# Every fourth piece of weights gets its low part from an accumulating DMA in a float32 encoder layer

## The chip, the cores and the metric

The kernel runs on one core of one Trainium2 chip. The metric is the device time of one execution in microseconds (us). The kernel before was timed twice: 2108.68 and 2109.56 us, median 2109.12 us.

## The reference

One encoder layer over 256 tokens of width 2048, all in float32:

```python
h = x + 0.5 * rms_norm(swiglu(rms_norm(x)))          # w_gate, w_up: 2048 x 5632, w_down: 5632 x 2048
u = rms_norm(h); q, k, v, f, g = split(u @ w_in)     # w_in: 2048 x 8192
y_attn = attention(q, k, v) @ w_attn_o               # 16 query heads, 4 key heads, rotary, head norms
y_four = real(fft2(f)) @ w_fourier                   # 8 groups of 128 channels
h = h + rms_norm((sigmoid(g_A) * y_attn + sigmoid(g_B) * y_four) @ w_out)
y = h + 0.5 * rms_norm(swiglu(rms_norm(h)))          # a second feed-forward half-step
```

Nearly all the work is in the matrix products with the weights: about 386 MB of float32 weights are read once, and each is used for 256 tokens.

## The kernel before, in words

**Precision.** TensorE multiplies in a format (fp32r) that keeps fewer bits than float32. So every operand is split in two: `hi` is the value rounded to fp32r, `lo` is what the rounding left. A product is three matmuls into one PSUM bank, hi by hi, hi by lo, lo by hi (`mm3`, lines 97 to 100; the weights' `lo` is the operand of line 99).

**Pieces of weights.** Weights are cut into chunks of 4 k-tiles by 512 columns, and a chunk into two pieces of 2 k-tiles: 128 partitions by 1024 float32 values, 512 KB. `piece` (line 104) loads a piece into a tile `raw` by a DMA of SyncE (SP), takes a `hi` and a `lo` tile, and calls `split` (line 92): ScalarE (ACT) copies `raw` to `hi` with rounding (line 93), then VectorE (DVE) writes `raw - hi` to `lo` (line 94). So `hi` and `lo` are ready one after the other, and `raw` is free when VectorE is done.

**Room.** There are 5 buffers for `raw` (`RAW_BUFS`) and 6 each for `hi` and `lo` (`RING`), used in turn. ScalarE can split a piece only when its load has landed and TensorE is done with the piece six places earlier. SP issues its DMAs in one queue, in order; the load of a piece waits until the `raw` buffer of the piece five places earlier is free, and the loads behind it in the queue wait with it.

**Stages.** `col_block` (line 179) computes 512 columns of u @ w for both tiles of 128 tokens: each piece serves 2 k-tiles by 2 token tiles by 3 matmuls, 12 matmuls in a row. `row_block` (line 209) adds ch @ w for one chunk, token tile 0 first and then token tile 1, so that the two pieces of a chunk are both used twice, 24 matmuls for the two. `ffn` (line 395) alternates two column blocks (gate, up) and a row block (down), 11 times. The mixers between the two half-steps use the same blocks.

**The two transitions.** At the end of the first half-step and of the mixers, `last_rows` (line 219) computes the last row block for token tile 0, then for token tile 1 while the norms of tile 0 run, then the first column block of what follows: token tile 0 while the norms of token tile 1 run, then token tile 1. The order on VectorE is written out by hand there. Part of the weights goes to spare room instead of the ring (`SPARE`, `SPARE_NEXT`); of the next column block's four chunks the first goes to a large buffer (tile names `wh`, `wl`), and the chunks 1 to 3 to the ring. Two pieces of these matter below: the first piece of chunk 1, and the first piece of chunk 3. Names there: `junk` are ScalarE's squares for the norms (line 336), `ca` to `cr` VectorE's steps of an inverse root (lines 148 to 159), `uh`, `ul` the split of the transposed next input, `pt` the PSUM tile of a transpose, `pc` and `pr` the PSUM tiles of a column and a row block. GpSimd (POOL) does only the products of the norms with their gains (line 337).

The order of instructions on each engine is set when the kernel is built: by the order of the code, by priorities of a scheduler for ScalarE, SP and TensorE, and by hand for VectorE in `last_rows`.

Of the kernel before, what the change touches and what calls it, by code (L numbers as in the profile page):

```python
# [10 lines left out]
F32 = mybir.dt.float32  # L11
# [3 lines left out]
AF = mybir.ActivationFunctionType  # L15
# [16 lines left out]
EPS = 1e-6  # L32
# [7 lines left out]
B8 = 8  # L40
CH = 3
WARM = 8
BY_POOL = ()


@with_exitstack
def encoder_layer(
# [41 lines left out]

    latest = {}  # L90

    def split(hi, lo, src):
        a = A.activation(hi, src, AF.Copy)  # L93
        v = V.tensor_tensor(out=lo, in0=src, in1=hi.bitcast(F32), op=ALU.subtract)  # L94
        latest["A"], latest["V"] = a.ins, v.ins
# [6 lines left out]
    ident = const.tile([P, P], F32, name="ident")  # L102

    def piece(src, k0, n, pools=None):
        """k-tiles k0 .. k0 + n of a chunk of weights: raw, hi, lo."""
        shape, part = [P, WP, NB], slice(0, n)
        raw = wraw.tile(shape, F32, tag="raw", name="raw")[:, part, :]
        load(raw, src.rearrange("p (k c) -> p k c", k=CK)[:, k0:k0 + n, :])
        pl, th, tl = pools or (wring, "hi", "lo")
        hi = pl.tile(shape, F32R, tag=th, name="whi")[:, part, :]  # L110
        lo = pl.tile(shape, F32R, tag=tl, name="wlo")[:, part, :]
        split(hi, lo, raw)
        return [(hi[:, k, :], lo[:, k, :]) for k in range(n)]

    def pieces(src, spare=None):
        """A chunk of weights, piece by piece: functions that load one and give (hi, lo) of its k-tiles.
        spare: the pool to take room from instead of the ring."""
        whole = {}

        def part(k0):  # L120
            if spare in (None, "chunk"):
                return piece(src, k0, WP, (chunk, "ch_hi", "ch_lo") if spare else None)
            if not whole:
                for c in ("h", "l"):
                    shape = [P, CK, NB]
                    whole[c] = big("w" + c, F32R, shape) if spare == "b8" else \
                        upool.tile(shape, F32R, tag=f"u{c}1", name=f"w{c}u")
            raw = wraw.tile([P, WP, NB], F32, tag="raw", name="raw")
            load(raw[:], src.rearrange("p (k c) -> p k c", k=CK)[:, k0:k0 + WP, :])
            hi, lo = (whole[c][:, k0:k0 + WP, :] for c in "hl")  # L130
            split(hi, lo, raw[:])
            return [(hi[:, j, :], lo[:, j, :]) for j in range(WP)]

        return [lambda k0=k0: part(k0) for k0 in range(0, CK, WP)]

    def weights(src, spare=None):
        """A chunk of weights as (hi, lo) of its k-tiles."""
        return [t for load_part in pieces(src, spare) for t in load_part()]

    def rsqrt_steps(ssq, n, inv, name, mult=1.0, pre=None):  # L140
        """mult / sqrt(ssq * inv + EPS), or of ssq * inv + pre: a step of third order and one of second."""
        up = (8.0 / 3.0 / mult) ** 2
        a, y, t, w, q, z, t2, w2, r = (small(name + c, n) for c in "aytwqzuvr")
        i = sm.tile([P, n], I32, tag="smi" + str(n), name=name + "i")
        if pre is None:
            yield r, V.tensor_scalar(out=a[:], in0=ssq, scalar1=inv * up, scalar2=EPS * up, op0=ALU.mult, op1=ALU.add)
        else:
            yield r, V.scalar_tensor_tensor(out=a[:], in0=ssq, scalar=inv * up, in1=pre, op0=ALU.mult, op1=ALU.add)
        yield r, V.tensor_scalar(out=i[:], in0=a[:].bitcast(I32), scalar1=1, scalar2=None, op0=ALU.logical_shift_right)
        yield r, V.tensor_scalar(out=y[:].bitcast(I32), in0=i[:], scalar1=-1.0, scalar2=float(0x5F3759DF),  # L150
                                 op0=ALU.mult, op1=ALU.add)
        yield r, V.tensor_tensor(out=t[:], in0=y[:], in1=y[:], op=ALU.mult)
        yield r, V.tensor_tensor(out=w[:], in0=t[:], in1=a[:], op=ALU.mult)
        yield r, V.scalar_tensor_tensor(out=q[:], in0=w[:], scalar=-10.0 / 3.0, in1=w[:], op0=ALU.add, op1=ALU.mult)
        yield r, V.scalar_tensor_tensor(out=z[:], in0=q[:], scalar=5.0, in1=y[:], op0=ALU.add, op1=ALU.mult)
        yield r, V.tensor_tensor(out=t2[:], in0=z[:], in1=z[:], op=ALU.mult)
        yield r, V.scalar_tensor_tensor(out=w2[:], in0=t2[:], scalar=-0.5 * 9.0 / 64.0, in1=a[:],
                                        op0=ALU.mult, op1=ALU.mult)
        yield r, V.scalar_tensor_tensor(out=r[:], in0=w2[:], scalar=1.5, in1=z[:], op0=ALU.add, op1=ALU.mult)

    def rsqrt(*args, **kw):
        for r, _ in rsqrt_steps(*args, **kw):
            pass
        return r
# [12 lines left out]
        return tuple(upool.tile([P, KD, P], F32R, tag=f"u{c}{t}", name=f"u{c}{t}") for c in "hl")  # L177

    def col_block(u, w, nb, between=()):
        """u @ w[nb] for both token tiles: PSUM tiles. between: pieces of other work, spread over the block."""  # L180
        ps = [pmm.tile([P, NB], F32, tag="mm", name="pc") for _ in range(NT)]
        step = KD / (len(between) + 1)
        done = 0
        for kg in range(KD // CK):
            wt = weights(w[nb, kg])
            for k in range(CK):
                kk = kg * CK + k
                if done < len(between) and kk >= (done + 1) * step:
                    if between[done]:
                        with tc.issue_after(mm.ins):  # L190
                            between[done]()
                    done += 1
                for t in range(NT):
                    mm = mm3(ps[t][:], u[t][0][:, kk, :], u[t][1][:, kk, :], *wt[k], kk == 0, kk == KD - 1)
        return ps
# [11 lines left out]
        return mm  # L207

    def row_block(ch, w, rb, y, first, between=()):
        """y += ch @ w[rb]; between[cb] comes ahead of column block cb."""  # L210
        for cb in range(D // NB):
            wt = weights(w[rb, cb])
            if cb < len(between) and between[cb]:
                with tc.issue_after(mm.ins):
                    between[cb]()
            for t in range(NT):
                mm = row_part(ch, wt, t, cb, y, first)

    def last_rows(ch, w, rb, y, norm, nxt=None, w_next=None):
        """The last row block, token tile 0 first, and the norms behind it; then the first column block of what  # L220
        follows, its token tile 0 while token tile 1 gets ready. VectorE's order is given: it has the most to do here."""
        ws = [weights(w[rb, cb], spare=SPARE[cb]) for cb in range(D // NB)]

        def row(t, cb):
# [92 lines left out]
        return a[:, cb * NB:(cb + 1) * NB]  # L317

    class PostNorm:
        """h += half * rms_norm(y) * g_post per token tile."""  # L320

        def __init__(self, y, h, g_post, half, store=None):
            self.y, self.h, self.g, self.half, self.store = y, h, g_post, half, store
# [35 lines left out]
                self.store(t, *self.parts[i])  # L359

    class NextInput:
        """u = transpose(h * g_pre), rs[t] = rsqrt(mean(h^2)); y is room."""

        def __init__(self, y, h, g_pre):
            self.y, self.h, self.g = y, h, g_pre
# [27 lines left out]
                yield  # L393

    def ffn(u, rs, wg, wu, wd, y, tail, gate0, w_next=None, early=()):
        """tail() loads what the end needs and gives what to do with y."""
        nblk = F // NB
        prev = None
        for f in range(nblk):
# [26 lines left out]
            prev = ch  # L426
        return last_rows(prev, wd, nblk - 1, y, norm, nxt, w_next), nxt

# [1 line left out]
    warm = small("warm", 1)  # L430
    V.memset(warm[:], 0.0)
    A.activation(warm[:], warm[:], AF.Silu)
# [36 lines left out]
    def tail():  # L469
        g_post, g_pre = bcast(f1_post, "gpost1"), bcast(mix_pre, "gpre1")  # L470
        return PostNorm(y, h, g_post, 0.5), NextInput(y, h, g_pre)
# [2 lines left out]
                  early=[lambda t=t: residual(t) for t in range(NT)])  # L474
    u, rs = nxt.u, nxt.rs

# [1 line left out]
    # column blocks of w_in: 0-3 q, 4 k, 5 v, 6-7 f, 8-11 gate A, 12-15 gate B  # L478
    spill = [nc.dram_tensor(f"h_spill{t}", [P, D], F32, kind="Internal").ap() for t in range(NT)]
    for t in range(NT):  # L480
        load(spill[t], h[t][:])
# [19 lines left out]
        tabs[nm] = (gc, gs)  # L501

    def norm_rope(ps, nm, t):
        """r * ps, RMS norm of each head, gain and rotation."""
        gc, gs = tabs[nm]
        q = work("q")
        ssq = small("ssq4", 4)
# [68 lines left out]
        return ah, al  # L576

    def fourier_channels(b, g, a):
        """Position 256 - k has the cosines of position k and its sines negated: both from positions 0 .. 128."""
        pb = ptr.tile([P, S + 2], F32, tag="tr", name="pb")  # L580
        for c, part in enumerate((slice(0, P + 2), slice(P + 2, S + 2))):
            cs = slice(c * P, (c + 1) * P)
# [47 lines left out]
            ps[t, hh] = p  # L630

    def attn_parts(j, ps, ch):
        """The products with v of the four heads of group j, each a part behind its transposes."""
        held, po = [], {}

        def turn_p(hh, i):
# [72 lines left out]
    norm, nxt = PostNorm(y, h2, g_post, 1.0), NextInput(y, h2, g_pre)  # L709

    def merged(cb, gz):
        """Column block cb of the gated sum, transposed: its room and the parts that fill it."""
        ch = new_chunk("mT")
        ms = []
        for t in range(NT):
# [18 lines left out]
        load(h2[t][:], spill[t])  # L734
    pg = last_rows(prev, w_out, 3, y, norm, nxt, f2_gate[0])

# [1 line left out]
    y = [big(f"yf{t}") for t in range(NT)]  # L738

    def store(t, lo, n):  # L740
# [74 lines left out]
```

## Time and profile before

| | |
|---|---|
| two timed runs | 2108.68 and 2109.56 us, median 2109.12 us |
| span of the profiled execution | 2107.7 us; that execution has no other time of its own here, and the median lies 1.4 us above its span |
| TensorE (PE) busy | 2089.4 us, 99% of the span, 9528 matmuls |
| VectorE busy | 1290.4 us, 61%; 885.9 us of it in 725 subtractions of line 94 for full pieces of weights |
| ScalarE busy | 971.3 us, 46% |
| GpSimd busy | 33.3 us, 2% |
| DMA | 404.61 MB by SP's queue, 59.1% of the 16 DMA engines' time |

The span runs from the first to the last instruction. A busy time is the time in which an engine has an instruction running; matmuls are pipelined, so that one lasts 390 ns though one starts every 0.23 us. The `idle before` of a group is the time its engine stood still ahead of it, with the engine whose signal ended the wait behind an arrow. The `us to landing` of a DMA runs from its issue until its data can be used. In the profile the lines of the kernel before are numbered as in the listing above; in the changed kernel the helpers stand 10 to 14 lines further down (line 94 is 104, line 93 is 103).

### The profile page before, as it was taken

How to read it: one execution, taken by the hardware profiler on the slowest of the kernel's cores; microseconds unless marked ns; L12 is line 12 of the kernel's file. 1: busy time of each engine (PE TensorE's matmuls, PEld its weight loads, DVE VectorE, ACT ScalarE, POOL GpSimd, SP SyncE). 2: the span in 40 equal slices, each digit the busy share in tenths (PEclk: the TensorE clock that was granted, in tenths of full speed). 3: DMA queues.
4: the chain of work that ended last, by engine and by line, in shares of the span. 5: the costliest groups of instructions: out<-in, count | busy, mean ns of one | idle time of the engine just before them, and what ended most of it. 6: DMA issues, size and time to landing. Idle time of an engine off the chain costs nothing.

```text
span 2107.7 us, 25198 instructions
## 1 busy us (share of the span) xinstructions
PE 2089.4 (99%) x9528; PEld 1729.8 (82%) x9528; DVE 1290.4 (61%) x1660; ACT 971.3 (46%) x1232; POOL 33.3 (2%) x30
## 2 busy tenths in 40 slices
PE   9999999999999999999999999999999999999998
PEld 7888888888888878888888888778888888888886
DVE  6655555555555786676767666875555555555556
ACT  7444444444444555555455444554444444444443
POOL 0000000000000100000000000200000000000001
PEclk9999999999999999999999999999999999999999
DMA  8665655665656566455545556556566556665563
GB/s 313 229 216 190 190 191 189 196 189 188 193 191 192 178 216 202 145 195 200 180 156 184 191 194 194 194 196 209 193 189 191 189 192 195 189 190 187 194 192 108
DMA packets 112874, 406.23 MB, mean 193 GB/s; under 512 B 12528, under 2 KB 14320, under 8 KB 111344
## 3 DMA queue, kind: packets, MB, share of 16 engines
q1 hardware_dynamic: 112752, 404.61, 59.1%
q8 instruction: 75, 1.23, 0.2%
q14 instruction: 47, 0.39, 0.1%
HBM read 400.37 MB, written 4.19 MB: 192 GB/s over the span
## 4 chain that ended last, share of the span: by engine, by line
PE 96%; DVE 3%; DMA 1%; issue 0%; ACT 0%; SPq 0%; DVEq 0%; ACTq 0%
PE pc L100 20%; PE pc L99 20%; PE pc L98 20%; PE pr L98 10%; PE pr L100 10%; PE pr L99 10%; PE pt L169 2%; PE pf L98 1%; PE pf L100 1%; PE pf L99 1%; DVE wlo L94 1%; DVE h L356 0%; PE pt L640 0%; DMA raw<-in_f_gate 0%; DVE y L206 0%
## 5 line engine op out<-in xcount | busy, mean ns | idle before, releaser
L94 DVE TENSOR_TENSOR wlo<-raw,whi 128x1024 fp32r<-128x1024 f32 (+1 forms) x727 | 887.3, 1221 | 741.9 <-ACT whi L93 741.6
L93 ACT ACTIVATE whi<-raw 128x1024 fp32r<-128x1024 f32 (+1 forms) x727 | 769.1, 1059 | 1009.7 <-PE pc L100 606.7
L98 PE MATMUL pc<-whi,uh 128*128 128x512 f32 x1904 | 744.2, 391 | 1.8 <-ACT uh L451 1.8
L100 PE MATMUL pc<-whi,ul 128*128 128x512 f32 x1904 | 741.6, 390 | 2.3 <-DVE ul L94 2.3
L99 PE MATMUL pc<-wlo,uh 128*128 128x512 f32 x1904 | 741.6, 390 | 2.2 <-DVE wlo L94 2.2
L100 PEld LDWEIGHTS pc<-whi,ul 128*128 128x128 f32 x1904 | 357.4, 188 | 77.6 <-DVE ul L94 3.2
L99 PEld LDWEIGHTS pc<-wlo,uh 128*128 128x128 f32 x1904 | 357.5, 188 | 76.7 <-DVE wlo L94 4.2
L98 PEld LDWEIGHTS pc<-whi,uh 128*128 128x128 f32 x1904 | 357.5, 188 | 76.0 <-ACT uh L451 3.4
L98 PE MATMUL pr<-whi,hTh 128*128 128x512 f32 x688 | 269.5, 392 | 0.0
L100 PE MATMUL pr<-whi,hTl 128*128 128x512 f32 x688 | 268.0, 389 | 0.0
L99 PE MATMUL pr<-wlo,hTh 128*128 128x512 f32 x688 | 267.7, 389 | 0.0
L100 PEld LDWEIGHTS pr<-whi,hTl 128*128 128x128 f32 x688 | 129.1, 188 | 27.0
L99 PEld LDWEIGHTS pr<-wlo,hTh 128*128 128x128 f32 x688 | 129.2, 188 | 26.2
L98 PEld LDWEIGHTS pr<-whi,hTh 128*128 128x128 f32 x688 | 129.2, 188 | 26.1
L206 DVE TENSOR_TENSOR yf<-pr,yf 128x512 f32<-128x512 f32 (+1 forms) x82 | 55.1, 672 | 10.4 <-PE pr L100 9.7
L206 DVE TENSOR_TENSOR y<-pr,y 128x512 f32<-128x512 f32 x80 | 54.7, 685 | 4.1 <-PE pr L100 3.6
L98 PE MATMUL pr<-whi,oTh 128*128 128x512 f32 x128 | 49.8, 389 | 0.0
L99 PE MATMUL pr<-wlo,oTh 128*128 128x512 f32 x128 | 49.8, 389 | 0.0
L100 PE MATMUL pr<-whi,oTl 128*128 128x512 f32 x128 | 49.8, 389 | 0.0
L98 PE MATMUL pr<-whi,mTh 128*128 128x512 f32 x120 | 46.9, 391 | 0.0
L100 PE MATMUL pr<-whi,mTl 128*128 128x512 f32 x120 | 46.7, 389 | 0.0
L99 PE MATMUL pr<-wlo,mTh 128*128 128x512 f32 x120 | 46.7, 389 | 0.0
(218 smaller groups left out, 1188.2 us busy)
## 6 DMA issues: line engine op xcount, KB each, us to landing
raw<-in_f_up SPq DMA_DIRECT2D x176, 512.0 KB, 4.7
raw<-in_f_down SPq DMA_DIRECT2D x176, 512.0 KB, 4.6
raw<-in_f_gate SPq DMA_DIRECT2D x175, 512.0 KB, 4.6
raw<-in_w_in SPq DMA_DIRECT2D x128, 512.0 KB, 4.4
raw<-in_w_ao SPq DMA_DIRECT2D x32, 512.0 KB, 3.9
raw<-in_w_out SPq DMA_DIRECT2D x32, 512.0 KB, 4.5
raw<-in_w_fo SPq DMA_DIRECT2D x16, 512.0 KB, 4.7
h<-in_x SPq DMA_DIRECT2D x2, 1024.0 KB, 8.6
```

What stands on the lines that cost most here:

```text
L93: a = A.activation(hi, src, AF.Copy)
L94: v = V.tensor_tensor(out=lo, in0=src, in1=hi.bitcast(F32), op=ALU.subtract)
L98: T.matmul(ps, lh, rh, start=first, stop=False)
L99: T.matmul(ps, lh, rl, start=False, stop=False)
L100: return T.matmul(ps, ll, rh, start=False, stop=last)
L169: T.transpose(pt[:, j, :], src[:, j * P:(j + 1) * P], ident[:])
L206: V.tensor_tensor(out=dst, in0=ps, in1=dst, op=ALU.add)
```

## The change

Calls of `piece` are counted. From the 33rd on, every fourth one (the 36th, the 40th and so on) is split in another way if its room is in the ring: ScalarE writes `hi` as before and then `lo = -raw`, rounded as `hi` is, so that `lo` is exactly `-hi`. A DMA issued by GpSimd then reads `raw`, adds it to what stands in `lo`, and writes the sum back: `raw - hi`, as before. VectorE has no part in these pieces. Pieces in spare room, the first 32 pieces, and all splits of other operands are unchanged.

```diff
+BY_DMA = 4
+BY_DMA_FROM = 32
...
+    turn_of = [0]
+
+    def split_by_dma(hi, lo, src):
+
+        A.activation(hi, src, AF.Copy)
+        A.activation(lo, src, AF.Copy, scale=-1.0)
+        nc.gpsimd.dma_start(lo.bitcast(F32), src, accum_op=ALU.add)
+
     def split(hi, lo, src):
         a = A.activation(hi, src, AF.Copy)
         v = V.tensor_tensor(out=lo, in0=src, in1=hi.bitcast(F32), op=ALU.subtract)
...
-        split(hi, lo, raw)
+        turn_of[0] += 1
+        if pools is None and turn_of[0] > BY_DMA_FROM and turn_of[0] % BY_DMA == 0:
+            split_by_dma(hi, lo, raw)
+        else:
+            split(hi, lo, raw)
         return [(hi[:, k, :], lo[:, k, :]) for k in range(n)]
```

173 pieces are treated so: VectorE's subtractions of full pieces `wlo` go from 725 to 552, ScalarE gets 173 more copies, GpSimd 173 DMAs. `DMAHW` in a row below is a wait for a load of SP's queue, `DMASW` one for a DMA of GpSimd; the digits name semaphores.

ScalarE in a feed-forward block, before (`whi` is the `hi` of a piece in the ring, the number behind a name is its buffer's own):

```order
L93 ACTIVATE whi_5278<-raw_5276 128x1024 [waits DMAHW1_49,DVE_49,PE_49]
L93 ACTIVATE whi_5284<-raw_5282 128x1024 [waits DMAHW2_49,DVE_49,PE_49]
L93 ACTIVATE whi_5332<-raw_5330 128x1024 [waits DMAHW3_49,DVE_49,PE_49]
L93 ACTIVATE whi_5338<-raw_5336 128x1024 [waits DMAHW4_49,DVE_49,PE_49]
L93 ACTIVATE whi_5344<-raw_5342 128x1024 [waits DMAHW5_49,DVE_49,PE_49]
```

The same pieces now:

```order
L99 ACTIVATE wlo_5334<-raw_5331 128x1024 [waits DMASW4_49,DMAHW1_49,DVE_49,PE_49]
L98 ACTIVATE whi_5333<-raw_5331 128x1024 [waits PE_49,Activation_49]
L103 ACTIVATE whi_5340<-raw_5338 128x1024 [waits DMAHW2_49,DVE_49,PE_49]
L103 ACTIVATE whi_5388<-raw_5386 128x1024 [waits DMAHW3_49,PE_49,Activation_49]
L103 ACTIVATE whi_5394<-raw_5392 128x1024 [waits DMAHW4_49,DVE_49,PE_49]
L99 ACTIVATE wlo_5401<-raw_5398 128x1024 [waits DMASW5_49,DMAHW5_49,DVE_49,PE_49]
L98 ACTIVATE whi_5400<-raw_5398 128x1024 [waits PE_49,Activation_49]
```

Every fourth piece has two copies, and the copy of `-raw` to `lo` is put ahead of that to `hi`.

SP at the first transition, now (`raw_5435` and `raw_5439` are the loads of the large buffer, `raw_5519` of the first piece of chunk 1, `raw_5727` and `raw_5736` of the two pieces of chunk 3):

```order
L76 DMA raw_5429<-in_f1_down 128x1024 [waits DMAHW6_49,DVE_49]
L76 DMA raw_5435<-in_w_in 128x1024 [waits DMAHW5_49,DMASW0_49]
L76 DMA raw_5439<-in_w_in 128x1024 [waits DMAHW7_49,DVE_49]
L76 DMA raw_5519<-in_w_in 128x1024 [waits DMAHW1_49,DVE_49]
L76 DMA raw_5631<-in_w_in 128x1024 [waits DMAHW2_49,DVE_49]
L76 DMA raw_5663<-in_w_in 128x1024 [waits DMAHW0_49,DVE_49]
L76 DMA raw_5694<-in_w_in 128x1024 [waits DMAHW3_49,DVE_49]
L76 DMA raw_5727<-in_w_in 128x1024 [waits DMAHW4_49,DVE_49]
L76 DMA raw_5736<-in_w_in 128x1024 [waits DMAHW5_49,DMASW1_49,Activation_49]
```

Before, all of these waited for VectorE alone. Now `raw_5435` waits until the accumulating DMA of a piece of the last row blocks has read its `raw`, and `raw_5736` until that of the first piece of chunk 1 has; 172 of SP's DMAs wait for one in this way.

ScalarE at the same transition, now, from the first piece of chunk 3 on:

```order
L98 ACTIVATE whi_5729<-raw_5727 128x1024 [waits DMAHW1_49,PE_49,Activation_49]
L103 ACTIVATE whi_5738<-raw_5736 128x1024 [waits DMAHW2_49,PE_49,Activation_49]
L350 ACTIVATE junk_5579,ssq1_2011<-y1_108 128x512 [waits DVE_49]
L103 ACTIVATE uh0_5603<-pt_5605 128x512 [waits PE_49]
...
L401 ACTIVATE junk_5680,ssn_5673<-h0_406 128x512 [waits Activation_49]
L103 ACTIVATE uh0_5603<-pt_5702 128x512 [waits PE_49]
L99 ACTIVATE wlo_5730<-raw_5727 128x1024 [waits DMASW0_49]
```

Here the copy of `-raw` of that piece is not beside the copy to `hi`: thirteen places and the whole of token tile 0's transposes (`uh`, four of them) lie between. The same happens at the second transition; at the other 171 pieces the two copies are at most two places apart.

## The prediction

> **What bounds the kernel now.** I read the page's engine table and chain first, then the waits of TensorE.
>
> ```profile
> span 2107.7 us, 25198 instructions
> ...
> PE 2089.4 (99%) x9528; PEld 1729.8 (82%) x9528; DVE 1290.4 (61%) x1660; ACT 971.3 (46%) x1232; POOL 33.3 (2%) x30
> ...
> PE 96%; DVE 3%; DMA 1%; issue 0%; ACT 0%; SPq 0%; DVEq 0%; ACTq 0%
> ...
> PE pc L100 <- DVE ul L94: 2.3, 2, 1.2
> PE pc L99 <- DVE wlo L94: 2.2, 3, 1.0
> PE pc L98 <- ACT uh L451: 1.8, 3, 1.3
> ```
>
> TensorE is the bound: 99% busy, and its longest waits in the whole run are a few of 1 us. At most 2107.7 - 2089.4 = 18.3 us (0.9%) could be won by any work on other engines, so VectorE's 61% is no limit. The question is only whether the new way of making `lo` is ever late. For that I read one steady stretch of the feed-forward and the groups of the split:
>
> ```profile
> 400.13 1.06 ACT L93 ACTIVATE whi<-raw 128x1024 fp32r<-128x1024 f32 x1 [1.66 <-PE pc L100]
> 402.85 1.06 ACT L93 ACTIVATE whi<-raw 128x1024 fp32r<-128x1024 f32 x1 [1.66 <-PE pc L100]
> ...
> 401.23 1.23 DVE L94 TENSOR_TENSOR wlo<-raw,whi 128x1024 fp32r<-128x1024 f32 x1 [1.49 <-ACT whi L93]
> ...
> 402.48 8.49 SPq L74 DMA_DIRECT2D raw<-in_f_down  x4
> ...
> L94 DVE TENSOR_TENSOR wlo<-raw,whi 128x1024 fp32r<-128x1024 f32 x725 | 885.9, 1223 | 737.5 <-ACT whi L93 737.2
> L93 ACT ACTIVATE whi<-raw 128x1024 fp32r<-128x1024 f32 x725 | 767.9, 1060 | 1007.1 <-PE pc L100 606.7 <-PE pr L100 323.2 <-DVE wlo L94 34.8
> ```
>
> One piece is split every 2.72 us, and ScalarE waits for TensorE to free a place in the ring (606.7 + 323.2 of its 1007.1 us of idle time there), not for a load. So splits run the full ring ahead: a piece is split when the sixth before it is done, and is needed after five more, 5 x 2.72 = 13.6 us later. In the row blocks the two pieces of a chunk are freed late:
>
> ```profile
> 2063.24 1.06 ACT L93 ACTIVATE whi<-raw 128x1024 fp32r<-128x1024 f32 x1 [3.02 <-PE pr L100]
> 2064.60 1.06 ACT L93 ACTIVATE whi<-raw 128x1024 fp32r<-128x1024 f32 x1 [0.30 <-PE pr L100]
> 2068.68 1.06 ACT L93 ACTIVATE whi<-raw 128x1024 fp32r<-128x1024 f32 x1 [3.02 <-PE pr L100]
> ```
>
> Pairs come every 5.44 us; a first piece is free after three quarters of its chunk and its place is needed three chunks on: 3 x 5.44 - 4.08 = 12.2 us.
>
> **The price of one accumulating DMA.** Call L the time from the end of the copy of `-raw` to the moment `lo` can be used and `raw` is free. The trace has no DMA of GpSimd and none that adds, so L is bounded by neighbours:
>
> ```profile
> q1 hardware_dynamic: 112752, 404.61, 59.1%
> ...
> raw<-in_f_up SPq DMA_DIRECT2D x176, 512.0 KB, 4.7
> ...
> h_spill<-h SPq DMA_DIRECT2D x2, 1024.0 KB, 3.8
> ...
> h<-h_spill SPq DMA_DIRECT2D x2, 1024.0 KB, 9.0
> ...
> L337 POOL TENSOR_TENSOR y<-y,gpost 128x512 f32<-128x512 f32 x8 | 11.3, 1437 | 731.4 <-ACT junk L336 731.4
> ```
>
> A load of 512 KB takes 4.7 us. The add must read 512 KB twice (`raw` and `lo`). 59.1% of 2107.7 us for 404.61 MB is 1.61 us of all 16 engines per 512 KB (0.524 MB), so the second read adds 1.6. GpSimd's part is unknown: between nothing and its longest kind of instruction here, 1.4 us; I take half, 0.7. L = 4.7 + 1.6 + 0.7 = 7.0 us. The ends: 3.8 (1 MB out of SBUF, no share for GpSimd) and 9.0 + 1.4 = 10.4 (1 MB loaded among other traffic). The middle is nearer to the plain load, which has the same queues and row lengths, so I keep 7.0.
>
> The Trainium skill (DMA: Bandwidth & Descriptors, Anatomy of one DMA — SWDGE (gpsimd) path) fits a GpSimd DMA with 2.0 us plus bytes over 436 GB/s; by it 1 MB of reads is an estimate of 4.4 us, L would be 4.4, and each stall below 2.6 us shorter. No run here shows a DMA of that path.
>
> **The change part by part.**
>
> *Removed:* 173 subtractions of 1.22 us on VectorE, 211 us. They lie beside TensorE's work, so they bring nothing in the steady stages.
>
> *Added on ScalarE:* 173 copies of 1.06 us, 183 us. ScalarE idles 1.66 us per 2.72 us ahead of its copy; one more every fourth piece fits. Worth 0.
>
> *Steady stages, the piece itself:* the copy to `lo` comes first, so `lo` is ready 1.06 + 7.0 = 8.1 us after the place is free, against 13.6 (column blocks) and 12.2 (row blocks). Hidden, up to L = 11.1.
>
> *Steady stages, the queue behind it:* `raw` is held L instead of a subtraction, and SP's queue stands still with it. The next such piece but one (eight pieces on) is loaded as the fourth in the queue, the held load being the first. So the loop is: copy 1.06, L, a load 4.7 and three more behind it at 1.6 each, then the same again: 10.6 + L per eight pieces, where TensorE takes 8 x 2.72 = 21.8. With L = 7.0 it is 17.6. The other accumulating DMA of these eight pieces shares the engines with those loads and can add its own transfer, up to 2 x 1.61 = 3.2: 20.8, still under. So L decides between 21.8 - 13.8 = 8.0 (all of the sharing) and 11.2 (none). The engines as a whole have room: 59.1% + 173 x 3.2 / 2107.7 = 85%. Worth 0, but with little to spare.
>
> *The transitions.* Here the ring is not ahead. The chain in order of time and the rows around it:
>
> ```profile
> 714.06 5.25 DMA raw<-in_w_in
> 719.33 1.07 ACT wh L93
> ...
> 707.05 1.06 ACT L93 ACTIVATE whi<-raw 128x1024 fp32r<-128x1024 f32 x1 [3.02 <-PE pr L100]
> ...
> 722.12 1.06 ACT L93 ACTIVATE whi<-raw 128x1024 fp32r<-128x1024 f32 x1 [0.41 <-DMA raw<-in_w_in]
> ...
> 727.11 0.60 DVE L148 SCALAR_TENSOR_TENSOR ca<-ssq,pre 128x1 f32<-128x1 f32 x1 [0.79 <-ACT junk L336]
> ...
> 744.53 0.58 ACT L93 ACTIVATE uh<-pt 128x512 fp32r<-128x512 f32 x1
> ...
> 747.98 1.22 DVE L94 TENSOR_TENSOR wlo<-raw,whi 128x1024 fp32r<-128x1024 f32 x1
> ...
> 749.25 0.50 PE L99 MATMUL pc<-wlo,uh 128*128 128x512 f32 x1 [1.02 <-DVE wlo L94]
> ...
> PE pt L169 <- DVE y L370: 0.5, 1, 0.5
> ```
>
> First, the loads of the large buffer. `raw_5435` now waits for the accumulating DMA of the piece that ScalarE split at 707.05: 707.05 + 1.06 + 7.0 = 715.1. The load behind it, which went out at 714.06 and ended ScalarE's wait at 719.33, follows, and lands 1.6 us after it: 715.1 + 4.7 + 1.6 = 721.4, 2.1 us late. The copy at 722.12 and the squares behind it on ScalarE, for which `ca` waits at 727.11, move with it, and TensorE already waits 0.5 us for `y` behind that chain. VectorE has one subtraction of 1.22 us less there; I take back half of that: 1.5 us late.
>
> Second, the first piece of chunk 3. Its copy of `-raw` stands behind the last `uh` of token tile 0, which ends at 744.53 + 0.58 = 745.1. So its `lo` is ready at 745.1 + 1.5 + 1.06 + 7.0 = 754.7, where TensorE now gets it at 749.25 (the subtraction ran at 747.98). That is 5.4 us of stall, the 1.5 included; nothing hides it, as the next matmul needs that `lo`. The second transition has the same row order. Two stalls: 10.8 us. With L = 3.8 the same sum gives 2 x 2.2 = 4.4, with L = 10.4 2 x 8.8 = 17.6. Of what is queued behind the waiting instructions: on POOL the norms' products follow the DMA of chunk 1 and wait only for its issue; on SP some loads of the next block wait for the DMA of chunk 3, and that block starts only after token tile 1's four runs of twelve matmuls, 4 x 2.72 = 10.9 us later.
>
> Sum, against the profiled execution: 2107.7 + 10.8 = 2118.5 of span, with the 1.4 us that the median lies above that span **2120 us**, 0.5% slower, which is less than the 2% that a measurement can tell from no change.
>
> **Rivals.**
>
> *The queue becomes the bound (slower).* If L is over the point above, the loop of `raw`, SP's queue and the add sets the pace of the 692 pieces (173 x 4). With L = 10 and 2.4 us of sharing: 10.6 + 10 + 2.4 = 23.0 instead of 21.8, 1.2 us more for each of 86.5 groups of eight, 107; the transitions cost 2 x 8.4 = 17. 2109 + 124 = 2233 us. For it: 85% of the engines' time, so bursts collide; the upper bound 10.4. Against it: the middle of the rows is 7.0.
>
> *GpSimd is held up by VectorE (slower).* The trace has the two engines hindering each other: the same one-element step takes five times as long beside GpSimd's products.
>
> ```profile
> 728.12 0.84 DVE L152 TENSOR_TENSOR ct<-cy 128x1 f32<-128x1 f32 x1
> ...
> 746.26 0.16 DVE L152 TENSOR_TENSOR ct<-cy 128x1 f32<-128x1 f32 x1
> ...
> 723.88 5.06 POOL L337 TENSOR_TENSOR y<-y,gpost 128x512 f32<-128x512 f32 x4 [723.43 <-ACT junk L336]
> ```
>
> If GpSimd has to wait out two subtractions while it writes a DMA's descriptors, L = 7.0 + 2 x 1.22 = 9.4; 10.6 + 9.4 + 2.4 = 22.4, 0.6 x 86.5 = 52 us, transitions 2 x 7.8 = 16: 2177 us. The rows show VectorE held up, not GpSimd's DMAs, so this has little. The Trainium skill (SBUF — State Buffer, SBUF: two separate sides) has this mechanism: a GpSimd DMA's descriptors cannot be written while VectorE runs an instruction in a two-port mode. It counts a subtraction of two tensors out of these modes (Who interferes with whom), so by it this kernel is spared; no run here shows it.
>
> *The transitions hide it too (no change).* VectorE loses two subtractions per transition, 2.3 us, and L near 3.8 leaves 2.2 of stall: 2107 to 2113, say 2110 us. Against it: TensorE's wait at 749.25 shows no slack at that very `lo`.
>
> *Faster by over 2%* would need 42 us; there are 18.3.
>
> **How the numbers follow.** Forecast (stalls at the transitions only, 2113 to 2128) 0.42; transitions hidden 0.16; queue the bound 0.35; GpSimd held up 0.06; faster 0.01. So faster 0.01, within 2% 0.58, slower 0.41. The predicted time is the forecast's 2120. The range reaches from 2107 (VectorE's relief, no stall) to 2245, past the queue's 2233, and leaves out its worse half.
>
> **What would show it.** Right: 173 more `wlo` copies on ScalarE, L of 6 to 8 us as the median to landing, no wait of TensorE for `wlo` between the transitions, two waits of about 5 us of line 99's matmul there. Wrong: TensorE's waits for the accumulating DMA repeated every eight pieces, SP's waits for it in hundreds of us, L over 9; or no wait at all.

## The result and the profile after

The changed kernel takes **2160.66 us** (median of two runs, 2160.31 and 2161.01) against 2109.12 before: the ratio is 1.0246, 95% interval 1.0229 to 1.0263. It is slower by 51.5 us, where 10.8 were forecast. The profiled execution took 2160.31 us with a span of 2158.5, 50.8 more than before.

First the page of the changed kernel: span, engines, the chain by engine and by line.

```profile
span 2158.5 us, 25704 instructions
...
PE 2107.4 (98%) x9528; PEld 1736.4 (80%) x9528; DVE 1085.9 (50%) x1487; ACT 1129.2 (52%) x1405; POOL 182.4 (8%) x203
...
PE 65%; DMA 27%; DVE 3%; ACT 3%; issue 2%; SPq 1%; POOL 0%; ACTq 0%; DVEq 0%; POOLq 0%
DMA wlo<-raw 15%; PE pc L109 13%; PE pc L110 13%; PE pc L108 13%; PE pr L109 7%; PE pr L110 7%; PE pr L108 7%; DMA raw<-in_f_down 4%; DMA raw<-in_f_gate 3%; DMA raw<-in_f_up 2%; DMA raw<-in_w_in 2%; ACT wlo L99 1%; PE pt L183 1%; SPq L76 1%; DVE wlo L104 1%
...
raw<-in_f_up SPq DMA_DIRECT2D x176, 512.0 KB, 5.7
raw<-in_f_down SPq DMA_DIRECT2D x176, 512.0 KB, 6.2
raw<-in_f_gate SPq DMA_DIRECT2D x175, 512.0 KB, 6.3
wlo<-raw POOLq DMA_DIRECT2D x173, 512.0 KB, 9.2
```

VectorE lost its 204 us (1290.4 to 1085.9) and ScalarE got 158 more, as the change says. But TensorE alone was 96% of the chain before, and now 27% of it are DMAs, 15% the accumulating ones. The accumulating DMA takes 9.2 us from issue to landing, not 7.0, and the loads beside it have become slower too, 5.7 to 6.3 us in the feed-forward blocks instead of 4.6 to 4.7. The waits of SP's queue, ScalarE and TensorE in the whole run (us in total, times, longest us) show where that arrives:

```profile
SPq L76 <- DMA wlo<-raw: 1272.0, 172, 11.5
SPq L76 <- DVE wlo L104: 337.2, 163, 13.0
```

```profile
ACT whi L103 <- PE pc L110: 191.2, 141, 3.0
ACT whi L103 <- DMA raw<-in_f_down: 127.8, 84, 3.6
ACT whi L103 <- DMA raw<-in_f_up: 123.3, 65, 5.1
ACT whi L103 <- DMA raw<-in_f_gate: 61.2, 52, 3.1
...
PE pc L109 <- DMA wlo<-raw: 14.9, 12, 3.9
PE pr L109 <- DMA wlo<-raw: 10.2, 11, 4.0
```

SP's wait by itself says little: before, it waited 1580 us for VectorE, without loss. ScalarE's rows say more. Before, it waited 929.9 us (606.7 + 323.2) for TensorE to free a place of the ring. Now it waits 191.2 for that in column blocks and 46.4 in row blocks ahead of `hi`, 73.2 and 56.2 ahead of the copies to `lo`, and over 300 us for loads. The ring is no longer full ahead, and so TensorE now sees a late `lo`, 23 times in these two rows alone.

**Where the 51 us lie.** Both kernels have 9528 matmuls, in the same order but for 56 places at the transitions, where TensorE's schedule puts transposes ahead of matmuls that wait for a late `lo`; they lie inside the stretches below. (In the experiments the order differs there too, or in the first 60 us.) I took the start of the n-th in each trace, and the difference says how far the changed kernel is behind at that point of the program. The columns below are stretches of the time of before; 60 to 640 is the first feed-forward block, 640 to 900 and 1320 to 1400 hold the transitions, 900 to 1320 the mixer, 1400 to 2110 the second feed-forward block. Each cell is what was lost in that stretch, in us, for this kernel and for all experiments below. What is lost up to 60 us is left out, for a reason that experiment 5 shows.

```
lost between, us       60-640  640-900  900-1320  1320-1400  1400-2060  2060-2110   sum
changed kernel            3.2     17.1       1.7       13.2       10.8        5.8  51.9
1 steady only             6.8      9.0       0.4        4.2        3.8        0.3  24.5
2 transitions only        0.0      6.9      -0.1        7.7        0.0        0.0  14.5
3 no late piece           3.5     13.0       1.5        7.0        8.2        2.6  35.8
4 every eighth            0.0      2.3       0.0        7.0        0.1        0.0   9.4
5 before, small x         0.0     -0.5       0.0       -0.3        0.0        0.0  -0.8
6 traffic only            0.0      0.2       0.0        2.0        0.0        0.0   2.2
7 hold only               0.0      0.6      -0.1        0.1        0.0        0.0   0.6
8 hold and traffic        0.0     -0.1       0.0       -1.1       25.9        2.7  27.5
9 hi added                0.0     10.9       1.9       20.2        0.0        0.0  33.0
10 six raw                0.0      7.5       1.9       10.6        0.1        1.1  21.2
11 transitions, hi added  0.0      8.2      -0.1       11.4        0.0        0.0  19.5
12 copy, not add          0.0      0.8      -0.1        7.5        0.0        0.0   8.3
```

30.3 us are lost in the two stretches with transitions and 21.6 in the rest. Two things have to be explained: why the steady stages lose anything, and why the transitions lose three times the forecast.

### The profile page after: what moved, and what is told of

Its sections match the earlier page's. It is cut to its first block, busy times and chain, and to the rows that moved or that the text cites. A ratio compares the mean times of both kernels' runs of the same rounds, so it can differ in the third digit from the quotient of the medians.

```text
span 2158.5 us, 25704 instructions
## 1 busy us (share of the span) xinstructions
PE 2107.4 (98%) x9528; PEld 1736.4 (80%) x9528; DVE 1085.9 (50%) x1487; ACT 1129.2 (52%) x1405; POOL 182.4 (8%) x203
## 3 DMA queue, kind: packets, MB, share of 16 engines
q0 software_dynamic: 24912, 90.71, 21.6%
## 4 chain that ended last, share of the span: by engine, by line
PE 65%; DMA 27%; DVE 3%; ACT 3%; issue 2%; SPq 1%; POOL 0%; ACTq 0%; DVEq 0%; POOLq 0%
DMA wlo<-raw 15%; PE pc L109 13%; PE pc L110 13%; PE pc L108 13%; PE pr L109 7%; PE pr L110 7%; PE pr L108 7%; DMA raw<-in_f_down 4%; DMA raw<-in_f_gate 3%; DMA raw<-in_f_up 2%; DMA raw<-in_w_in 2%; ACT wlo L99 1%; PE pt L183 1%; SPq L76 1%; DVE wlo L104 1%
## 5 line engine op out<-in xcount | busy, mean ns | idle before, releaser
L104 DVE TENSOR_TENSOR wlo<-raw,whi 128x1024 fp32r<-128x1024 f32 (+1 forms) x554 | 676.0, 1222 | 896.9 <-ACT whi L103 894.9
L103 ACT ACTIVATE whi<-raw 128x1024 fp32r<-128x1024 f32 (+1 forms) x554 | 584.5, 1057 | 642.2 <-PE pc L110 191.2
L109 PEld LDWEIGHTS pc<-wlo,uh 128*128 128x128 f32 x1904 | 358.8, 188 | 94.0 <-DMA wlo<-raw 20.8
L99 ACT ACTIVATE wlo<-raw 128x1024 fp32r<-128x1024 f32 x173 | 183.4, 1060 | 268.2 <-PE pc L109 73.2
L100 POOL DMA_DIRECT2D wlo<-raw x173 | 149.4, 864 | 1914.4 <-ACT wlo L99 1710.9
L98 ACT ACTIVATE whi<-raw 128x1024 fp32r<-128x1024 f32 x173 | 180.4, 1043 | 1.9 <-DMA raw<-in_f_gate 0.8
```

The costliest lines, as they stand in the source:

```text
L99: A.activation(lo, src, AF.Copy, scale=-1.0)
L100: nc.gpsimd.dma_start(lo.bitcast(F32), src, accum_op=ALU.add)
L109: T.matmul(ps, lh, rl, start=False, stop=False)
```

## The experiments

All ratios are to the kernel before, in runs on the same chip (2108.0 to 2108.8 us).

**1 and 2: the two halves of the change.** A flag is set in `last_rows`: for the last row block, for the first column block behind it, and at the end of the kernel.

```diff
+    in_last = [False]
-        if pools is None and turn_of[0] > BY_DMA_FROM and turn_of[0] % BY_DMA == 0:
+        if pools is None and turn_of[0] > BY_DMA_FROM and turn_of[0] % BY_DMA == 0 and not in_last[0]:
```

Experiment 1 has `not in_last[0]` (166 pieces), experiment 2 `in_last[0]` (7 pieces).

> The changed kernel, but in the last row blocks and the first column block behind them (the transitions and the end) every piece is split by VectorE as before. Theory A (each stage pays for itself: the transitions lose by the late copy of chunk 3's first piece and by loads that wait, 24 of the 51 us that were lost, the end 3): about 2134 us. Theory B (the steady stages drain the ring, and the transitions only show that debt): the transitions stay bad, over 2150 us.

> The other half: only pieces of the last row blocks and the first column blocks behind them go by DMA, all others are split by VectorE as before. Theory A: 2109 + 27 = about 2136 us, with the waits of 4 us for the late piece of chunk 3 at both transitions. Theory B: the ring is full when a transition comes, so little is lost, under 2118 us.

Measured: 2134.85 us (1.0113, interval 1.009 to 1.0136) and 2124.4 us (1.007, 1.0055 to 1.0085). Both halves cost something, 26.0 and 15.6 us; the whole costs 51.5, 10 more than the two together. (The four runs of experiment 1 spread from 2124.81 to 2136.0 us, so the 10 is rough.) The steady pieces have a price that was forecast as nothing, and they make the transitions worse: experiment 1 loses 13.2 us in the two stretches with transitions, though no piece of a transition goes by DMA.

In the second, the group of TensorE's matmuls with `wlo` and the landing of its seven DMAs:

```profile
L110 PE MATMUL pc<-wlo,uh 128*128 128x512 f32 x1904 | 743.2, 390 | 8.1 <-DMA wlo<-raw 8.0
...
wlo<-raw POOLq DMA_DIRECT2D x7, 512.0 KB, 5.9
```

The late first piece costs 8.0 us in two waits of 3.9 and 4.0. What stands around the first of them, in order of time:

```profile
751.28 0.63 PE L184 MATMUL pt<-ident,y 128*128 128x128 f32 x4 [1.68 <-DVE y L388]
755.82 0.80 PE L110 MATMUL pc<-wlo,uh 128*128 128x512 f32 x1 [3.91 <-DMA wlo<-raw]
756.41 0.63 PE L111 MATMUL pc<-whi,ul 128*128 128x512 f32 x1
...
759.40 0.40 PE L109 MATMUL pc<-whi,uh 128*128 128x512 f32 x1
759.64 0.40 PE L110 MATMUL pc<-wlo,uh 128*128 128x512 f32 x1
```

The matmuls behind the wait take 0.63 us each until 759, and then 0.40: from 755.82 to 759.40 eight are started, which at the later pitch (759.64 - 759.40 = 0.24) need 1.9 us instead of 3.6. Ahead of them TensorE had stood still from 749.60 to 755.82 but for four short transposes, 6.2 us; that pause costs 1.7 us more afterwards. By the same comparison of starts TensorE is 1.4 us behind at 739.76 already (it waited 0.67 us for `y` at 737.72), 4.95 at the matmul that waits, and 6.9 behind the slow ones.

**3: without the late piece.** VectorE splits the first piece of chunk 3 at each transition; all other pieces are as in the change.

```diff
-        if pools is None and turn_of[0] > BY_DMA_FROM and turn_of[0] % BY_DMA == 0:
+        if pools is None and turn_of[0] > BY_DMA_FROM and turn_of[0] % BY_DMA == 0 and not late[0]:
+            late[0] = (kg, i) == (3, 0)
```

> The changed kernel, but the first piece of chunk 3 of the column block at each transition (whose copy of -raw stands thirteen places late on ScalarE) is split by VectorE. If the late copy costs its wait alone (3.9 and 3.8 us): 2160.7 - 8 = about 2153 us. If each such wait also brings TensorE to half its clock for the 3.4 to 6.8 us that the changed kernel's trace shows right behind (1.7 to 3.4 us lost each): about 2147 us. If the loads that wait are the cause: no change, 2158 us or more.

Measured: 2149.97 us (1.0202, 1.0185 to 1.0219), 10.7 less than the changed kernel. Its profiled execution was the fastest of its runs (2145.18 us); in it the table has 4.1 us less at the first transition (17.1 to 13.0), 6.2 less at the second, and 5.8 less in the second feed-forward block. The median lies between the two forecasts for a costly late piece (2153 for the wait alone, 2147 with slow matmuls behind it), and 20 us are still lost in the two stretches without it.

**4: every eighth piece.** `BY_DMA = 8`.

> Every eighth piece by DMA in place of every fourth, otherwise the changed kernel (at the first transition only the first piece of chunk 1 then goes by DMA, at the second only the late one of chunk 3). If the loss comes by the loop of raw, SP's queue and the accumulating DMA, in which two DMAs per eight pieces meet: the steady loss of 24 us vanishes nearly, 2109 + 2 + 10 to 14 = about 2122 us. If it goes by the bytes that the added DMAs move: half of it stays, 2109 + 26 = 2135 us.

Measured: 2118.25 us (1.0044, 1.0029 to 1.0059). 7.0 of its 9.4 us lie at the second transition, where the late piece is still one of the eighths, and its steady stages lose 0.1. So with half as many DMAs not half of the steady loss is left, but none of it: what costs is no price for each DMA. VectorE is relieved of 86 subtractions here (639 instead of 725 full ones), and the steady stages gain nothing from it.

**5 to 8: what the DMA does to others.** In the steady stages an accumulating DMA does three things: it delays its own `lo`, it occupies `raw` and with it SP's queue, and it takes time of the DMA engines, about as much as two plain transfers (experiment 12). In these kernels VectorE makes every `lo` again, and at the 166 places of experiment 1 GpSimd does one of the other two things, or both, to a dummy tile. Its room comes from the pool that loads `x`, which experiment 5 alone shrinks.

```diff
-    xpool = pool("xpool", 3)
+    xpool = pool("xpool", 1)
```

```diff
-        A.activation(hi, src, AF.Copy)
-        A.activation(lo, src, AF.Copy, scale=-1.0)
-        nc.gpsimd.dma_start(lo.bitcast(F32), src, accum_op=ALU.add)
+        split(hi, lo, src)
+        nc.gpsimd.dma_start(dummy[:], hi.bitcast(F32), accum_op=ALU.add)
```

That is experiment 6, traffic only. In 7, hold only, the last line is

```diff
+        nc.gpsimd.tensor_copy(dummy[:, 0, 0:1], hi.bitcast(F32)[:, 0, 0:1])
+        for _ in range(HOLD):
+            nc.gpsimd.memset(dummy[:], 0.0)
+        nc.gpsimd.tensor_copy(dummy[:, 0, 0:1], src[:, 0, 0:1])
```

with `HOLD = 8`, and in 8, with both, it is

```diff
+        nc.gpsimd.dma_start(dummy[:], src, accum_op=ALU.add)
```

> The kernel before with one buffer instead of three in the pool that loads x, the room that the next three kernels need for a dummy tile. A control: 2109 us (ratio 0.999 to 1.001) if the pool is of no weight; else what it costs has to be taken off the next three.

> VectorE makes every lo again, but at the 166 places of the first experiment GpSimd sends a 512 KB DMA that adds hi to a dummy tile: its result is used by nothing, no load waits for it, and raw is free after the subtraction. This leaves only the traffic. Traffic theory (loads that land 1 to 2 us later starve the split by themselves): 2125 to 2135 us, as in the first experiment (2134.85). Hold theory (SP's queue stands still until the add has read raw): 2109 to 2113. Theory of the late lo (TensorE waits for the lo of that very piece): 2109 to 2113. Interaction theory (a held queue and slower loads together): 2109 to 2115, loads near 5.5 us.

> VectorE makes every lo, and at the same 166 places GpSimd keeps raw occupied: after hi it writes a dummy tile eight times and then reads one column of raw, by an estimate from its products of 128x512 (1.4 us) some 9 us in all. No traffic is added; SP's queue is held as long as by the accumulating DMA. Hold theory: 2125 to 2135 us, and SP waits for GpSimd in hundreds of us. Traffic theory and late lo: 2109 to 2113. Interaction theory: 2109 to 2115, because without the slower loads a loop of 10.6 + 9 = 19.6 us fits into 21.8.

> VectorE makes every lo, and at the same 166 places GpSimd sends the very DMA of the change (raw, added) to a dummy tile: the traffic and the held raw of the change without the late lo. Hold theory, traffic theory and interaction theory: 2128 to 2136 us, as the first experiment. Theory of the late lo: 2109 to 2115.

Measured: the control 2126.48 us (1.0087, 1.0072 to 1.0102), so the small pool costs 18.4 us by itself, all of it in the first 60 us. Against that control: traffic only 2128.22, +1.7; hold only 2127.37, +0.9; both 2155.4, **+28.9**. Neither alone is worth 2 us; together they cost about what experiment 1 cost (26.0). So traffic with a held queue is enough for a loss, as the interaction theory has it, even where no `lo` comes from a DMA. That the two sums are alike is luck, as the rows of experiment 8 show below.

The hold was as long as the DMA's. GpSimd's groups in experiment 7, and SP's wait there:

```profile
L103 POOL MEMSET dummy<- 128x1024 f32 x1328 | 1268.7, 955 | 76.8
L101 POOL COPY dummy<-whi 128x1 f32<-128x1 f32 x166 | 180.6, 1088 | 432.9 <-ACT whi L107 432.4
L104 POOL COPY dummy<-raw 128x1 f32<-128x1 f32 x166 | 39.6, 239 | 10.5
```

```profile
SPq L77 <- POOL dummy L104: 368.4, 157, 4.4
```

1.1 + 8 x 0.96 + 0.2 = 9.0 us, yet SP waits for it 368.4 us in all and never over 4.4: the loads behind are quick (3.7 to 3.9 us in the feed-forward blocks), so the queue is back ahead each time. The traffic alone has these rows in experiment 6:

```profile
q1 hardware_dynamic: 112752, 404.61, 54.8%
q0 software_dynamic: 23904, 87.04, 25.7%
...
dummy<-whi POOLq DMA_DIRECT2D x166, 512.0 KB, 7.0
```

The engines are over 80% busy and nothing is lost, so their total is not the bound. With both, in experiment 8:

```profile
dummy<-raw POOLq DMA_DIRECT2D x166, 512.0 KB, 8.4
```

```profile
SPq L76 <- DMA dummy<-raw: 789.4, 145, 11.2
```

The same 87 MB take longer, 8.4 instead of 7.0 us. That the held loads go out at once and meet the next DMA would explain it, but the start differs too: in experiment 6 GpSimd waits for ScalarE's `hi`, in 8 for the landing of the load alone, so its DMA starts earlier than that of the change. And TensorE waits for something else:

```profile
POOL dummy L100 <- DMA raw<-in_f_down: 476.8, 38, 96.9
```

```profile
PE pr L108 <- ACT sg L430: 19.0, 7, 4.1
```

Seven waits for `sg`, the activation of the gate, make up most of the 25.9 us. In ScalarE's order `sg` stands behind copies that wait for loads. In experiment 1 and in the changed kernel TensorE waits for the accumulating DMA itself, 7.5 us in 13 waits and 25.1 in 23. There the late `lo` is the last link of the chain; experiment 8 shows only that it is not the only one by which late loads can reach TensorE. What makes the `lo` late is the question of 9 and 10.

**9 and 10: taking the hold away from the change.** Experiment 9 adds `hi` to minus `raw`, so `raw` is free once ScalarE has copied it (`lo` has the other sign then). Experiment 10 gives the change a sixth `raw` buffer (and the small pool for `x`).

```diff
-        nc.gpsimd.dma_start(lo.bitcast(F32), src, accum_op=ALU.add)
+        nc.gpsimd.dma_start(lo.bitcast(F32), hi.bitcast(F32), accum_op=ALU.add)
```

```diff
-RAW_BUFS = 5
+RAW_BUFS = 6
-    xpool = pool("xpool", 3)
+    xpool = pool("xpool", 1)
```

> The changed kernel, but its DMAs add hi, not raw, to minus raw: lo comes out with the other sign (another result). Traffic, L and the two copies stay; raw is free once ScalarE has copied it, so SP's queue is not held by the DMA. Interaction theory: only the transitions' cost is left, 2120 to 2128 us, and TensorE's steady stages as before. Traffic theory and late lo: 2145 to 2161 (the changed kernel has 2160.7).

> The changed kernel with six raw buffers instead of five (and one buffer for x, which cost 18.4 us by itself, and partly the same early stall). Interaction theory: the held load gets one more buffer ahead, so most of the steady 26 us go and the sum is 2109 + 18 + 16 to 22 for the transitions: 2143 to 2152 us. If the queue were no matter: 2160 + 18 = 2178, or 2165 if the early stalls overlap.

Measured: 2142.98 us (1.0163, 1.0146 to 1.018) and 2147.65 us (1.0185, 1.0169 to 1.02). The second is inside its forecast, the first 15 us over it. The table says where: in both, the steady stages lose nothing (0.0 and 0.1 us between 1400 and 2060, where the change loses 10.8), but in experiment 9 the transitions lose 31.1. One long window of the second feed-forward block (1640 to 2060 us), with TensorE's busy time and matmuls, granted clock, DMA share and GB/s, first before, then the changed kernel, then 9 and 10:

```profile
1640.00:2060.00 420.00, 420.00 (x1878) 1.00 0.60 191
```

```profile
1640.00:2060.00 420.00, 415.38 (x1849) 1.00 0.83 235
```

```profile
1640.00:2060.00 420.00, 420.00 (x1878) 1.00 0.85 239
```

```profile
1640.00:2060.00 420.00, 420.00 (x1883) 1.00 0.84 238
```

With 85% and 84% of the DMA engines' time taken TensorE still starts as many matmuls as before; with 83% and a held `raw` it starts 29 fewer, 29 x 0.22 (420 / 1878) = 6.5 us. In experiment 9 TensorE's longest waits at the transitions are these:

```profile
756.54 0.79 PE L109 MATMUL pc<-wlo,uh 128*128 128x512 f32 x1 [5.27 <-DMA wlo<-whi]
...
781.66 0.50 PE L109 MATMUL pc<-wlo,uh 128*128 128x512 f32 x1 [2.77 <-DMA wlo<-whi]
...
1360.34 0.79 PE L109 MATMUL pr<-wlo,mTh 128*128 128x512 f32 x1 [5.58 <-DMA wlo<-whi]
...
1400.74 0.80 PE L109 MATMUL pc<-wlo,uh 128*128 128x512 f32 x1 [5.83 <-DMA wlo<-whi]
1426.76 0.79 PE L109 MATMUL pc<-wlo,uh 128*128 128x512 f32 x1 [3.23 <-DMA wlo<-whi]
```

So freeing `raw` settles the steady stages, and only them. The DMAs still take 8.0 us to landing in experiment 9 and 9.0 in 10, against 9.2, and in both `lo` still comes from them. So between 1400 and 2060 us neither the long way of `lo` nor the traffic costs anything unless the loads are held as well.

**11: the transitions without the held loads.** Experiment 2 with the line of experiment 9.

> The second experiment (DMA pieces in the last rows alone, 2124.4) with hi added to minus raw instead of raw, so that no load at the transitions waits for a DMA (the sign of lo is turned: another result). If the late loads cost 1.5 us at each transition as forecast: 2121 to 2122 us. If the late first piece is all of it: 2124, as before.

Measured: 2126.02 us (1.0085, 1.0069 to 1.01), not faster than experiment 2 but about 1.6 slower. It does not price the late loads, because something else moved:

```profile
wlo<-whi POOLq DMA_DIRECT2D x7, 512.0 KB, 9.1
```

In experiment 2 the median of these seven DMAs was 5.9 us. The two that TensorE waits for landed after 8.5 and 8.3 us there and after 10.3 and 10.3 here, and its waits grew from 3.9 and 4.0 to 5.7 and 6.1: as much as the landings. That they take longer because the loads are free to go out beside them is argued; no run shows it by itself.

**12: copy, not add.** Experiment 4 with a DMA that only copies `raw` over `lo` (`lo` is `raw` then).

```diff
-        nc.gpsimd.dma_start(lo.bitcast(F32), src, accum_op=ALU.add)
+        nc.gpsimd.dma_start(lo.bitcast(F32), src)
```

> The fourth experiment (every eighth piece, 2118.25, median 5.8 us from issue to landing) with a DMA that copies raw over lo and adds nothing (lo is raw then: another result). If the add reads both sides one after the other, as forecast: 5.8 - 1.6 = 4.2 us to landing, half the engines' time, and 2112 to 2116 us. If the add is made in the same pass: 5.5 to 5.8 us and the same time.

Measured: 2114.81 us (1.0032, 1.002 to 1.0043). Its rows, and behind them those of experiment 4:

```profile
q0 software_dynamic: 12384, 45.09, 5.3%
...
wlo<-raw POOLq DMA_DIRECT2D x86, 512.0 KB, 4.4
```

```profile
q0 software_dynamic: 12384, 45.09, 11.2%
...
wlo<-raw POOLq DMA_DIRECT2D x86, 512.0 KB, 5.8
```

The add costs 1.4 us of landing (0.33 of it in GpSimd's instruction, 0.86 us against 0.53) and twice the engines' time: 11.2% of 2117.1 us over 86 is 2.76 us of all 16 engines for each DMA, against 1.30 for the copy. The page counts the bytes once in both, so the bytes don't show the add; the share of time does.

## Why the prediction was wrong

The sign was right, and so was the late `lo` at the transitions. The step that failed is the queue loop of the steady stages, which was put at 17.6 us, at most 20.8, against 21.8, and priced at nothing.

*What bounds the kernel, and the removed subtractions:* right. Experiments 4, 6, 7, 9 and 10 show steady stages that lose at most 3.1 us and gain nothing, though in 4, 9 and 10 VectorE has 86 to 173 subtractions less.

*The price L,* a term of that step. It was put together as load 4.7 + second read 1.6 + GpSimd 0.7 = 7.0. The parts were fair: the add is 1.4 in all (experiment 12), and GpSimd's part 0.86, the median of its instruction, from the changed kernel's rows of the tile (ns, least, median and most):

```profile
L100 POOL DMA_DIRECT2D wlo<-raw x173: 850/859/1002, 88.1 to 2117.1; - x173
```

Where the DMAs are few, the sum is 5.8, even less than 7.0. But 7.0 was then used as a constant while the change itself set the traffic. Beside its own kind and a held queue the same DMA takes 9.2, and the loads 5.7 to 6.3. The Trainium skill (DMA: Bandwidth & Descriptors, Anatomy of one DMA — SWDGE (gpsimd) path) gives, as estimates by its fit, 4.4 us for 1 MB of reads and 3.2 for 0.5 MB. The trace's medians of 5.8 and 4.4 lie 1.4 and 1.2 above it where the DMAs are few, and 9.2 is more than twice its figure.

*The queue loop of 10.6 + L against 21.8 us:* the step that failed. The loop exists as it was drawn; two of its terms were too small. In the timelines of the changed kernel it can be followed from one accumulating DMA to the next but one. Between 1400 and 2060 us (55 cases; medians, which add up only roughly) the held load is issued 0.05 us after the DMA has landed, and the fourth load lands 11.9 us later, where 4.7 + 3 x 1.6 = 9.5 were forecast. The copy takes 1.06 and the issue 0.35, and L is 9.9 there, not 7.0: 23.3 us from landing to landing. TensorE's pace before is 22.06 per eight pieces (66.2 us for a block of 24, transposes included). 38 of the 55 loops are over it; single DMAs land after anything from 4.5 to 12.7 us. In 42 of the 55 ScalarE's copy to `lo` starts within 0.3 us after its load has landed, in experiment 10 in 5 of 55, in experiment 9 in none of 56. Its waits for loads ahead of that copy in this stretch, in the changed kernel (36 waits, 64.3 us) and behind it the longer of the two in experiment 10 (5.1 us):

```profile
ACT wlo L99 <- DMA raw<-in_f_gate: 26.6, 14, 3.2
ACT wlo L99 <- DMA raw<-in_f_down: 20.6, 12, 3.6
...
ACT wlo L99 <- DMA raw<-in_f_up: 17.1, 10, 2.9
```

```profile
ACT wlo L99 <- DMA raw<-in_f_up: 2.9, 1, 2.9
```

Experiment 10 has the same L (9.8 in this stretch) and loads as slow (6.3 to 6.6), and loses nothing here; so it is the loop through `raw`, not L by itself. "Worth 0, but with little to spare" was read as a safe zero. Experiments 6 and 7 show traffic and hold without loss, 9 and 10 the change with the hold removed or eased and no steady loss. When the loss starts is not settled: experiment 8 runs 1400 us without any and loses 25.9 in the next 660, the changed kernel loses some in every stretch.

*The rival "the queue becomes the bound":* it had the right cause and a price five times too high. Its loop of 23.0 us is close to the measured median of 23.3. But it charged every group of eight the full difference, 107 us; shorter loops lie between the long ones, 17 of the 55, and the steady stages lost 21.6.

*GpSimd held up by VectorE:* not seen. Its instruction takes 850 to 1002 ns in all 173 cases, with VectorE busy half of the time (DVE 50%), where the rival added 2.4 us.

*The transitions:* two stalls of 5.4 us, 3.9 for the late piece and 1.5 for late loads, were forecast. Taken alone (experiment 2) TensorE fell 1.4 us behind ahead of the first late piece, and 3.6 more at it. Both sizes fit, and partly by luck. The load that was to come 2.1 us late was nearly on time (the second copy to `wh` starts at 719.78 us, before at 719.33), and in experiment 11, where no load is held, TensorE falls behind by 1.1 us in the same place; what delays `y` there is open. The late piece landed after 8.5 us, not 7.0, but part of that wait was filled: TensorE's schedule in the changed kernels puts four transposes ahead of the matmul that waits, which the forecast did not see. Missing was what follows a stall. The granted clock around it in the changed kernel:

```profile
755.00:760.00 5.00, 0.63 (x4) 0.74 0.82 196
760.00:765.00 5.00, 4.02 (x11) 0.58 0.55 179
```

After two waits with four transposes between them the clock is granted at 0.58 in the next 5 us. Alone (experiment 2) that cost 1.7 us behind the first late piece; taken for both, as an estimate, it is 3.4 of the 14.5. The Trainium skill (TensorE: Matmul & The Clock Gate, What's actually happening) says that TensorE falls to half its clock after an idle window of some 3.4 us and comes back after as long a busy one. The traces agree only in part. Matmuls of 0.6 to 0.8 us follow the pauses of 6.2 us and, in experiment 9, of 5.58 and 3.23; behind the one of 3.98 below they begin 1.4 us later; and none follow the ones of 2.19 below and 2.77 in experiment 9. But they also follow a pause of 2.65 at the end of the changed kernel, and none follow one of 3.50 in experiment 8:

```profile
2126.81 0.79 PE L109 MATMUL pr<-wlo,hTh 128*128 128x512 f32 x1 [2.65 <-DMA wlo<-raw]
```

```profile
1889.99 0.50 PE L108 MATMUL pr<-whi,hTh 128*128 128x512 f32 x1 [3.50 <-ACT sg L430]
```

The window runs freely, says the Trainium skill in the same section, which may be why the length of a pause alone does not tell. A forecast of 5.4 us stalls should have priced it.

*The transitions in the full change:* 30.3 us instead of 14.5. Most of the difference is the failed step again: with a sixth `raw` buffer and all 173 DMAs the same stretches lose 18.1, and experiment 1 loses 13.2 there without a DMA in the transitions themselves. A ring that is not full ahead when it arrives at a transition has no slack for the late piece or for the chain to `y`. In the last row blocks of the mixer the changed kernel has a wait, the third row, that neither the forecast nor experiment 2 has. Experiments 9 and 10 have it too (5.58 and 3.69 us), so the held loads alone don't explain it, and its cause stays open:

```profile
738.81 0.63 PE L183 MATMUL pt<-ident,y 128*128 128x128 f32 x4 [2.19 <-DVE y L384]
...
760.98 0.80 PE L109 MATMUL pc<-wlo,uh 128*128 128x512 f32 x1 [3.94 <-DMA wlo<-raw]
...
1367.26 0.50 PE L109 MATMUL pr<-wlo,mTh 128*128 128x512 f32 x1 [3.98 <-DMA wlo<-raw]
```

*What would show it:* of the signs named for "wrong", two came true (L over 9, SP's waits in hundreds of us), and one in part: TensorE does wait for the DMA, 23 times, but not every eight pieces. Of those for "right", the 173 copies and waits of about 4 us at the transitions came.

No version here beats the kernel before: the nearest that makes the same `lo` is experiment 4 at 1.0044.

## What to carry to other kernels

A transfer that holds a buffer of a load queue is not priced by its own length alone: sum the loop of buffer, queue and transfer, with durations as they will be beside the new traffic, and compare it with the pace of the bound engine. Here it was put at 17.6 to 20.8 us against 21.8 and came out at 23.3; with so little to spare, forecast a loss and test it by easing one side: one more buffer, or a source that is held anyway. A stall of a few microseconds on TensorE is charged with the slow matmuls behind it too.

## What the runs showed of the hardware

- An accumulating DMA of 512 KB within SBUF took 2.76 us of all 16 DMA engines (experiment 4), a plain one 1.30 (experiment 12), and the page's bytes are the same for both.
- Accumulating DMAs of that size landed after a median of 5.8 us (every eighth piece), 7.0 and 8.0 (every fourth, no load held; experiments 6 and 9), 8.4 to 9.2 (every fourth, with held loads), and 9.1 where only seven of them met unheld loads (experiment 11).
- In the window of 1640 to 2060 us, 85% and 84% of the DMA engines' time was taken in experiments 9 and 10 without any loss on TensorE.
- A pause of 6.2 us on TensorE was followed by 3.6 us of matmuls of 0.63 us each, one of 2.65 us by 6.1 us of them; pauses of 2.19, 2.77 and 3.50 us by none.
- The pool for `x` with one buffer instead of three cost 18.4 us at the start.
